# Seven products in place of eight for gate and up, and feed-forward outputs in parts

## The chip, the cores and the metric

The kernel runs on one core of a Trainium2 chip. The metric is the device time of one execution in microseconds. The core has five engines that run side by side: TensorE (PE in the profile, its weight loads PEld) for matrix products, VectorE (DVE) and ScalarE (ACT) for elementwise work, GpSimd (POOL), and SyncE (SP), from whose queue most DMA transfers are issued here. TensorE writes into eight PSUM banks of 128 x 512 floats; everything else lies in SBUF.

## The reference

Two encoder layers over 512 tokens of width 1024, in float32. Each layer is attention and then a feed-forward network with 2816 hidden units; the change touches only the second.

```python
def swiglu(h, w_gate, w_up, w_down):
    return (jax.nn.silu(h @ w_gate) * (h @ w_up)) @ w_down

def reference(x, norm_mix, norm_ffn, w_qkv_a, w_out_a, sink_a, w_qkv_b, w_out_b,
              w_gate, w_up, w_down, norm_final):
    for i in range(DEPTH):
...
        h = rmsnorm(x, norm_ffn[i])
        x = x + swiglu(h, w_gate[i], w_up[i], w_down[i])
    return rmsnorm(x, norm_final)
```

## The kernel before

The state x lies transposed in SBUF: NK = 8 blocks of 128 features by 512 tokens. Every float32 operand of a product is split in two: a high half, rounded by a ScalarE copy, and a low half, the difference, by VectorE (`split`, L91). A product is then three passes, high by high, high by low and low by high (`mm3`, L113), each in matmuls of 128 x 128 weights by 256 tokens. The weights come as units of 128 x 1024 (eight blocks of 128 x 128), and `weight_tiles` (L95) gives each three tiles: wraw, filled by a DMA on SP's queue, and wh and wl, its halves. All three have three buffers (`wpool`, L71), shared by every unit of the kernel.

`swiglu` (L494) runs once a layer, for 22 blocks f of 128 hidden units. For each f `gate(f)` and `up(f)` are units of eight steps (one step is one block of features, six matmuls), with xh and xl, the halves of x times its gain, as moving operand. The norm's factor per token, the row norm["rb"], is applied afterwards: `norm_sums` (L256) adds up squares over features by matmuls with a column of ones and works out the factors, `norm_rows` (L265) turns them into a row by transposes and a copy. `combine(f)` multiplies both products by that row, applies Silu, multiplies, and splits the result into ah and al, which hold all 22 blocks.

Then eight output blocks j: three weight pieces (8, 8 and 6 blocks f), 22 x 6 matmuls into one bank, and the sum with x. In layer 0 `residual` (L278) adds, writes the operands of the next layer's products (`operands`, L211, into xh and xl, here in an order of token classes) and squares x for the next norm (`squares`, L221), whose sum GpSimd keeps. In layer 1 the last j goes through `final` (L450): the last product is made in two halves of 256 tokens, and the norm and the output of the first half (`sums(0)`, `leave(0)`) are put between the matmuls of the second.

The order on TensorE is the order of the program text. On the other engines a planner orders the instructions when the program is built: among those that it finds ready, the earlier in the program goes first; a tile gets a buffer when one of its name is free.

Of the kernel before, what the change touches and what calls it, by code (L numbers as in the profile page):

```python
# [14 lines left out]
S = 512  # L15
# [8 lines left out]
WIN_A = 128  # L24
SLOPES = [float(np.float32(2.0) ** np.float32(-8.0 * (h + 1) / H)) for h in range(H)]
# [39 lines left out]
def trunk(ctx, tc, xT, gains, sink, tabs, qsc, wunits, wv, outT):  # L65
# [385 lines left out]
    def final(product, ps0, ps1, n, j):  # L451
# [30 lines left out]
        for k, _ in enumerate(gen):  # L482
            if k == 5:
                run(sums(0))
            elif k == 12:
                leave(0)
# [7 lines left out]
    def swiglu(u, n):  # L494
        with tc.tile_pool(name="ffn", bufs=2) as pool:
            ah = pool.tile([128, NF, S], F32R, name="ah", bufs=1)
            al = pool.tile([128, NF, S], F32R, name="al", bufs=1)
            part = {}

            def gate(f):  # L500
                def done(ps):
                    part["g"] = ps
                return unit(u + 2 * f, xh, xl, ("mm", "sc")[f % 2], done)

            def up(f):
                def done(ps):
                    part["u"] = ps
                return unit(u + 2 * f + 1, xh, xl, ("tp", "mm")[f % 2], done)

            def combine(f):  # L510
                gs = pool.tile([128, S], F32, name="gs")
# [5 lines left out]
                split(ah[:, f, :], al[:, f, :], us)  # L517

            for f in range(NF):
                if f == 0:  # L520
                    run(gate(0)[1])
                    norm_sums()
                    run(up(0)[1])
                    norm_rows()
                else:
                    run(gate(f)[1])
                    run(up(f)[1])
                combine(f)
            u += 2 * NF
            for j in range(NK):  # L530
                w = []
                for c0 in (0, 8, 16):
                    nk = min(8, NF - c0)
                    w.append(load_unit(wunits[u][:, :128 * nk], (nk, 128)))
                    u += 1
                def product(ps, cols, w=w):
                    for f in range(NF):
                        wh, wl = w[f // 8]
                        mm3(ps[:, cols], wh[:, f % 8], wl[:, f % 8], ah[:, f, cols], al[:, f, cols],
                            f == 0, f == NF - 1)  # L540
                        yield

                ps = bank(("mm", "sc")[j % 2])
                if n < 4:
                    run(product(ps, slice(0, S)))
                    residual(j, ps, n)
                elif j < NK - 1:
# [411 lines left out]
```

## Time and profile before

| what | us |
|---|---|
| median of 3 runs | 1472.62 (1472.39 to 1474.02) |
| the profiled execution | 1473.99 |
| its span, first to last instruction | 1472.3 |
| layer 0, first product of the norm sums ahead of gate and up | 192.48 |
| layer 0, down: first matmul | 427.6 |
| layer 1, last gate and up operands written | 1341.6 |
| layer 1, last down matmul starts | 1460.0 |

The page of the profile gives each engine's busy time and the chain of work that ended last. A row of grouped instructions has line, engine, operation, the tile written and the tiles read, shapes and count; then busy time and mean duration in ns; then the idle time of the engine before them and what ended it. A row of the timeline has start, duration, engine, line and tiles. A row of stretches has the stretch, its length, then busy time and count of PE, PEld, DVE, ACT and POOL, the granted clock of TensorE (1.00 is full), the busy share of the DMA engines and GB/s. A row of one tile has shortest, median and longest duration in ns. A row of DMA issues has the count, the size and the median time to landing.

### The profile page before, as it was taken

Reading aid. Unit: us, or ns where it says so; the run is one execution under the profiler, and the core shown is the slowest. Engines: PE = TensorE matmul, PEld = TensorE weight load, DVE = VectorE, ACT = ScalarE, POOL = GpSimd, SP = SyncE. Lnnn points to the kernel's source line nnn. Section 1 sums busy time; section 2 is a strip of 40 time slices with the busy share of each in tenths; the row PEclk is TensorE's granted clock in tenths of the full one; section 3 lists DMA queues with packets and bytes.
Section 4 is the critical chain, followed back from the end, with each engine's and each line's share of the span. In section 5 each row is a group of like instructions: output and inputs, shape, how many; then the busy total and the mean of one; then the engine's idle time right before and its main releaser. Section 6 shows DMA issues by size and latency. Waiting matters only on the chain.

```text
span 1472.3 us, 29609 instructions
## 1 busy us (share of the span) xinstructions
PE 1453.9 (99%) x12820; PEld 1426.7 (97%) x12820; DVE 732.6 (50%) x1400; ACT 613.9 (42%) x1126; POOL 109.1 (7%) x152
## 2 busy tenths in 40 slices
PE   8999999999999999999999999999999999999997
PEld 8988999999999999999999999999999999999997
DVE  6776544444443345346556556556464444443223
ACT  6776433322323335445545536536343322332221
POOL 3334200000000010000000000000030000000111
PEclk9999999999999999999999999999999999999998
DMA  6110232323223232312212122222132322232331
GB/s 201 58 59 15 87 101 87 101 101 100 94 87 104 94 111 69 101 63 86 79 67 87 58 87 73 72 87 73 44 116 86 101 101 98 90 101 91 96 103 57
DMA packets 38450, 128.29 MB, mean 87 GB/s; under 512 B 4528, under 2 KB 6832, under 8 KB 38320
## 3 DMA queue, kind: packets, MB, share of 16 engines
q1 hardware_dynamic: 36832, 125.08, 25.5%
q8 instruction: 100, 1.64, 0.4%
q10 hardware_dynamic: 1488, 1.33, 0.3%
q14 instruction: 30, 0.25, 0.1%
HBM read 124.29 MB, written 2.10 MB: 86 GB/s over the span
## 4 chain that ended last, share of the span: by engine, by line
PE 94%; DVE 2%; ACT 2%; issue 1%; DMA 0%; POOL 0%; SPq 0%; DVEq 0%; ACTq 0%; POOLq 0%
PE mm L118 51%; PE sc L118 16%; PE psv L118 10%; PE tp L118 8%; PE sc L696 1%; PE sc L637 1%; PE ov L378 1%; PE ov L751 1%; PE sc L140 1%; PE tp L364 1%; PE tp L659 1%; PE ov L678 1%; ACT pr L353 0%; DVE qt L128 0%; PE tp L738 0%
## 5 line engine op out<-in xcount | busy, mean ns | idle before, releaser
L92 ACT ACTIVATE wh<-wraw 128x1024 fp32r<-128x1024 f32 (+3 forms) x239 | 247.6, 1037 | 599.6 <-PE mm L118 252.0
L93 DVE TENSOR_TENSOR wl<-wraw,wh 128x1024 fp32r<-128x1024 f32 (+3 forms) x239 | 290.2, 1215 | 203.3 <-ACT wh L92 202.7
L118 PE MATMUL mm<-xh,wh 128*128 128x256 f32 x1632 | 331.4, 284 | 0.4 <-ACT xh L217 0.4
L118 PE MATMUL mm<-xh,wl 128*128 128x256 f32 x1632 | 321.6, 279 | 2.6 <-DVE wl L93 2.6
L118 PE MATMUL mm<-xl,wh 128*128 128x256 f32 x1632 | 321.7, 279 | 0.7 <-DVE xl L218 0.6
L118 PEld LDWEIGHTS mm<-xh,wh 128*128 128x128 f32 x1632 | 248.5, 189 | 6.3 <-issue 4.8
L118 PEld LDWEIGHTS mm<-xh,wl 128*128 128x128 f32 x1632 | 247.9, 189 | 3.2 <-DVE wl L93 3.2
L118 PEld LDWEIGHTS mm<-xl,wh 128*128 128x128 f32 x1632 | 248.5, 189 | 1.4 <-DVE xl L218 1.3
L232 POOL TENSOR_TENSOR ssum<-ssum,tmp 128x512 f32<-128x512 f32 x34 | 53.7, 1581 | 994.4 <-ACT tmp L228 979.9
L118 PE MATMUL psv<-wh,xh 128*128 128x256 f32 x288 | 82.8, 287 | 0.0
L118 PE MATMUL psv<-wl,xh 128*128 128x256 f32 x288 | 80.4, 279 | 0.0
L118 PE MATMUL psv<-wh,xl 128*128 128x256 f32 x288 | 80.3, 279 | 0.0
L118 PE MATMUL mm<-ah,wh 128*128 128x256 f32 x374 | 74.9, 277 | 0.0
L118 PE MATMUL mm<-al,wh 128*128 128x256 f32 x374 | 74.7, 276 | 0.0
L118 PE MATMUL mm<-ah,wl 128*128 128x256 f32 x374 | 74.7, 276 | 0.0
L118 PE MATMUL tp<-xh,wh 128*128 128x256 f32 x352 | 68.8, 277 | 0.0
L118 PE MATMUL sc<-xh,wh 128*128 128x256 f32 x352 | 68.7, 277 | 0.0
L118 PE MATMUL tp<-xh,wl 128*128 128x256 f32 x352 | 68.6, 276 | 0.0
L118 PE MATMUL tp<-xl,wh 128*128 128x256 f32 x352 | 68.6, 276 | 0.0
L118 PE MATMUL sc<-xh,wl 128*128 128x256 f32 x352 | 68.5, 276 | 0.0
L118 PE MATMUL sc<-xl,wh 128*128 128x256 f32 x352 | 68.5, 276 | 0.0
L118 PE MATMUL sc<-ah,wh 128*128 128x256 f32 x330 | 66.0, 276 | 0.0
(175 smaller groups left out, 2728.6 us busy)
## 6 DMA issues: line engine op xcount, KB each, us to landing
wraw<-wunits SPq DMA_DIRECT2D x192, 512.0 KB, 3.2
wraw<-wv SPq DMA_DIRECT2D x26, 512.0 KB, 3.3
wraw<-wunits SPq DMA_DIRECT2D x16, 384.0 KB, 3.0
x<-xT SPq DMA_DIRECT2D x8, 256.0 KB, 5.1
wraw<-wunits SPq DMA_DIRECT2D x3, 256.0 KB, 5.5
outT<-x ACTq DMA_DIRECT2D x2, 384.0 KB, 2.7
tab<-tabs SPq DMA_DIRECT2D x1, 512.0 KB, 5.5
outT<-x ACTq DMA_DIRECT2D x2, 256.0 KB, 2.2
```

What stands on the lines that cost most here:

```text
L92: nc.scalar.activation(out_h, src, AF.Copy)
L93: nc.vector.tensor_tensor(out_l, src, out_h.bitcast(F32), op=OP.subtract)
L118: nc.tensor.matmul(out[:, cols], a, b[:, cols], start=first and k == 0 and c == 0, stop=last and k == 2, skip_group_check=True)
L140: nc.tensor.matmul(outs[a], qp[a][:, qc], k[a][:, kc], start=first and k is kp, stop=k is low, skip_group_check=True)
L232: nc.gpsimd.tensor_tensor(norm["sum"], norm["sum"], sq, op=OP.add)
L364: nc.tensor.transpose(tp[:, 256 * hf + 128 * i:256 * hf + 128 * i + 128], st["pr"][:, 2 * i + hf, 128 * kb:128 * kb + 128], ident)
L378: nc.tensor.matmul(ov[64 * hf:64 * hf + 64, :256], v0[:, k0 // 128 + kb, vs], st["pt", kb][:, 256 * hf:256 * hf + 256], start=(kb == 0), s ...
L637: nc.tensor.matmul(out, qk["qs", p][a][:, 128 * t:128 * t + 128], kp[k], start=t == ts[0] and k == 0, stop=k == 1, skip_group_check=True)
L659: nc.tensor.transpose(tp[:, (nb * a + kb) * 128:(nb * a + kb) * 128 + 128], st["pr", p, ts][:, a, o + 128 * kb:o + 128 * kb + 128], ident)
L678: nc.tensor.matmul(ov[rows, 128 * t - 64:128 * t + 64], v[:, t - 1 + kb, vs], pt[:, 256 * a + 128 * kb:256 * a + 128 * kb + 128], start=Fa ...
L696: nc.tensor.matmul(ps[a][:, o:o + 128], qk["q", p, 1 + g][rows, cols], qk["k", p, 1 + g][rows, cols], start=(o == 0), stop=True, skip_grou ...
L751: nc.tensor.matmul(ov[rows, 128 * c:128 * c + 128], vals[p // 2, 1 + g][:, c, hv + 64 * a:hv + 64 * a + 64], pts[g][:, 256 * a + 128 * (c ...
```

## The change

The first four f's (`plain`) stay as they were. While they run, the normed input x times gain times norm["rb"] is written out, cut into quarters (B11, B12, B21, B22: the halves of the features by the halves of the tokens), and from these four combinations T1 to T4 are made; B11, B21, B22 and T1 to T4 are split into bh and bl (`input_steps`). For each of the other 18 f's, gate and up together are taken as a 2 x 2 block product (two outputs by two halves of the features, times two halves of the features by two halves of the tokens). `strassen` makes it from seven products of 12 matmuls in place of eight, in two PSUM banks, with copies to SBUF between. Its weights are: the two halves of the gate unit (1 and 2), the sums 4 and 6, of which each is one plain load and one adding DMA issued by GpSimd, the sums 5 and 7, added by VectorE from these, and the second half of the up unit (3). `strassens` lays the products of successive f's into each other.

The hidden outputs no longer stand side by side: ah and al hold 3 blocks, and xh and xl, free after the plain f's, hold 8. So the f's are taken in parts, (0-10), (11-18), (19-21) in layer 0 and (0-10), (11-21) in layer 1, and after each part its down products are added to x. The weights of the down products are laid out by part. Some steps of a part's first down product are put between the last products of the part.

```diff
+PARTS = ((0, 11), (11, 19), (19, NF)), ((0, 11), (11, NF))
...
-            if k == 5:
+            if k == 4:
                 run(sums(0))
-            elif k == 12:
+            elif k == 10:
                 leave(0)
...
-            ah = pool.tile([128, NF, S], F32R, name="ah", bufs=1)
-            al = pool.tile([128, NF, S], F32R, name="al", bufs=1)
+            ah = pool.tile([128, 3, S], F32R, name="ah", bufs=1)
+            al = pool.tile([128, 3, S], F32R, name="al", bufs=1)
...
+            def input_steps():
...
+                        nc.vector.scalar_tensor_tensor(raw[k][:, j % 4, :], x[:, j, cols], g_sb[:, n - 1, j:j + 1],
+                                                       norm["rb"][:, cols], op0=OP.mult, op1=OP.mult)
...
+                steps = [lambda j=j: normed(j) for j in range(NK)]
+                steps += [lambda: parts(B11), lambda: less(T1, B11, B12), lambda: parts(B21), lambda: parts(T1),
+                          lambda: less(T2, T1, B22, -1.0), lambda: parts(T2), lambda: less(T3, B22, B12),
+                          lambda: parts(T3), lambda: less(T4, T2, B21, -1.0), lambda: parts(T4), lambda: parts(B22)]
+                return steps
+
+            def loads(f):
+
+                g, v = wunits[u0 + 2 * f], wunits[u0 + 2 * f + 1]
+                sums = pool.tile([128, 1024], F32, name="w64")
+                nc.sync.dma_start(sums[:, 0:512], g[:, 0:512])
+                nc.sync.dma_start(sums[:, 512:1024], v[:, 512:1024])
+                for k in range(2):
+                    nc.gpsimd.dma_start(sums[:, 512 * k:512 * k + 512], v[:, 0:512], accum_op=OP.add)
+                raw = wpool.tile([128, 1024], F32, name="wraw")
+                nc.sync.dma_start(raw, g)
+                last = pool.tile([128, 512], F32, name="w3")
+                nc.sync.dma_start(last, v[:, 512:1024])
+                return raw, sums, last
+
+            def weights(raw, sums, last):
...
+                halves((wpool, "wh", "wl"), (1, 2), raw)
+                far = pool.tile([128, 1024], F32, name="w57")
+                nc.vector.tensor_tensor(far[:, 0:512], sums[:, 512:1024], raw[:, 0:512], op=OP.add)
+                nc.vector.tensor_tensor(far[:, 512:1024], far[:, 0:512], raw[:, 512:1024], op=OP.add)
+                halves((pool, "h57", "l57"), (5, 7), far)
+                halves((wpool, "wh", "wl"), (6, 4), sums)
+                halves((pool, "h3", "l3"), (3,), last, 512)
+                return w
...
+                def s0():
+                    v["a"], v["g"] = bank("mm"), pool.tile([128, S], F32, name="gs", bufs=3)
+                    product(v["a"][:, one], w[1], B11, True)
+                    nc.scalar.activation(v["g"][:, one], v["a"][:, one], AF.Copy)
...
+                def s6():
+                    product(v["a"][:, one], w[6], T3, False)
+                    v["u"] = pool.tile([128, S], F32, name="us")
+                    nc.scalar.activation(v["u"][:, two], v["a"][:, one], AF.Copy)
+                    nc.vector.tensor_tensor(v["u"][:, two], v["b"][:, two], v["u"][:, two], op=OP.add)
...
+                def s11():
+                    product(v["b"][:, two], w[7], B22, False)
+                    g, t = v["g"], v["u"]
+                    nc.vector.tensor_tensor(g, v["b"], g, op=OP.add)
+                    nc.scalar.activation(g, g, AF.Silu)
+                    nc.vector.scalar_tensor_tensor(t[:, one], v["a"][:, one], -1.0, g[:, one], op0=OP.mult, op1=OP.mult)
+                    nc.vector.scalar_tensor_tensor(t[:, two], t[:, two], -1.0, g[:, two], op0=OP.mult, op1=OP.mult)
+                    split(*place(f), t)
...
+            def strassens(fs, ws, fill, early):
+
+
+                order = sorted((7 * i + at, i, at) for i in range(len(fs)) for at in (0, 1, 3, 5, 6, 9, 11))
+                steps = {}
+                for _, i, at in order:
+                    f = fs[i]
+                    if at == 0:
+                        steps[i] = strassen(f, ws.pop(f))
+                    steps[i][at]()
+                    if at == 1 and i + 1 < len(fs):
+                        ready(f + 1, min(f + 2, fs[-1]))
+                    if i == len(fs) - 1 and at >= 6:
+                        for _ in range(3):
+                            if early:
+                                early -= 1
+                                next(fill)
+
+            def down(j, fs, first):
...
+                w = []
+                for c0 in range(0, len(fs), 8):
+                    m = min(8, len(fs) - c0)
+                    w.append(load_unit(wunits[first + j * len(range(0, len(fs), 8)) + c0 // 8][:, :128 * m], (m, 128)))
+                return gen
...
+            gen = up(0)[1]
+            for _ in range(5):
+                next(gen)
+            norm_rows()
+            run(gen)
+            combine(0)
+            steps = input_steps()
+            ws = {}
+            for f in range(1, plain):
+                for k, (_, gen) in enumerate((gate(f), up(f))):
+                    for i, _ in enumerate(gen):
+                        if i % 2 and steps:
+                            steps.pop(0)()
+                    if f == plain - 1 and k == 0:
+                        ready(plain, plain + 1)
                 combine(f)
...
+            for p, (f0, f1) in enumerate(parts):
+                fs = list(range(f0, f1))
+                pieces = -(-len(fs) // 8)
+                gens = {0: down(0, fs, at)}
+                ps = bank("tp")
+                fill = gens[0](ps, slice(0, S))
+                strassens([f for f in fs if f >= plain], ws, fill, len(fs) - 1)
+                for j in range(NK):
+                    if j:
+                        gens[j] = down(j, fs, at)
+                        ps = bank(("mm", "sc")[j % 2])
+                        fill = gens[j](ps, slice(0, S))
+                    if j == NK - 1 and f1 < NF:
+                        ready(f1, f1 + 1)
...
-    nc = _bacc.Bacc("TRN2", target_bir_lowering=False, num_devices=1)
+    nc = _bacc.Bacc("TRN2", target_bir_lowering=False, num_devices=1, dynamic_dma_scratch_size=4096)
```

`ready(f, ahead)` issues `loads` up to ahead and calls `weights(f)`.

131 lines of the change are left out of this document (91 added, 40 removed).

## The prediction

> **What bounds the kernel now.** I read the page's busy shares and chain first, then the busy time by stage, because the change touches only the two feed-forward stages.
>
> ```profile
> span 1472.3 us, 29609 instructions
> ...
> PE 1453.9 (99%) x12820; PEld 1426.7 (97%) x12820; DVE 732.6 (50%) x1400; ACT 613.9 (42%) x1126; POOL 109.1 (7%) x152
> ...
> PE 94%; DVE 2%; ACT 2%; issue 1%; DMA 0%; POOL 0%; SPq 0%; DVEq 0%; ACTq 0%; POOLq 0%
> ```
> ```profile
> 204.00:427.00 223.00, 223.00 (x1970) 223.00 (x1970) 103.26 (x123) 67.39 (x82) 0.00 (x0) 1.00 0.29 97
> 427.00:547.00 120.00, 120.00 (x1062) 120.00 (x1061) 41.77 (x41) 36.69 (x39) 9.60 (x6) 1.00 0.29 95
> ```
>
> TensorE has 12820 matmuls and as many weight loads and is never idle in a feed-forward stage: in 204 to 427 us (gate and up) it is busy 223.00 of 223.00 us at full clock, and in 427 to 547 (down) 120.00 of 120.00. So 1970 matmuls in 223.00 us make **113.2 ns** each, and whatever removes one there saves that much, as long as nothing else becomes late. VectorE is busy 46% of the first stretch (103.26), ScalarE 30%. They are the cover that the change spends.
>
> **The products removed.** Plain gate and up take 16 x 3 x 2 = 96 matmuls of 256 columns for one f; seven products of 4 x 3 take 84. Every matmul already has a weight load of its own, so another stationary operand each time costs nothing new. 12 x 113.2 ns = 1.36 us for each of 18 f's in 2 layers: **-48.9 us**. The down matmuls stay the same in number.
>
> **VectorE before the first seven-product f.** Prices:
>
> ```profile
> L93 DVE TENSOR_TENSOR wl<-wraw,wh 128x1024 fp32r<-128x1024 f32 x41 | 50.1, 1223 | 4.8 <-ACT wh L92 4.8
> L92 ACT ACTIVATE wh<-wraw 128x1024 fp32r<-128x1024 f32 x41 | 43.8, 1067 | 140.1 <-issue 73.2 <-PE sc L118 32.0 <-PE mm L118 31.0
> ...
> L93 DVE TENSOR_TENSOR al<-us,ah 128x512 fp32r<-128x512 f32 x21 | 14.4, 686 | 0.7 <-ACT ah L92 0.7
> L516 DVE TENSOR_TENSOR us<-us,gs 128x512 f32<-128x512 f32 x20 | 13.9, 693 | 2.1
> L514 ACT ACTIVATE gs<-gs 128x512 f32<-128x512 f32 x21 | 12.9, 614 | 0.0
> L92 ACT ACTIVATE ah<-us 128x512 fp32r<-128x512 f32 x20 | 12.7, 635 | 12.7 <-DVE us L516 12.7
> ```
> ```profile
> L382 ACT ACTIVATE oh<-ov x16: 362/367/387, 58.5 to 153.6; 128x256 fp32r<-128x256 f32 x16
> L383 DVE TENSOR_TENSOR ol<-ov,oh x16: 406/424/426, 58.9 to 154.0; 128x256 fp32r<-128x256 f32 x16
> ```
>
> A 1024-wide two-input operation is 1.22 us, a 512-wide one 0.69, a 256-wide one 0.42. All the new input work waits for the row norm["rb"]. This is where that row stands now:
>
> ```profile
> 192.48 0.94 PE L236 MATMUL ssq<-ones,ssum 128*128 128x1 f32 x8
> 198.83 0.60 PE L270 MATMUL rrow<-ident,rstd 128*128 128x128 f32 x4
> ```
> ```profile
> 198.85 1.06 ACT L92 ACTIVATE wh<-wraw 128x1024 fp32r<-128x1024 f32 x1 [3.82 <-issue]
> 199.81 0.58 ACT L273 ACTIVATE rb<-rrow 128x512 f32<-128x512 f32 x1
> ...
> 204.74 1.07 ACT L92 ACTIVATE wh<-wraw 128x1024 fp32r<-128x1024 f32 x1 [0.91 <-PE sc L118]
> ```
> ```profile
> 204.92 0.69 DVE L513 TENSOR_TENSOR gs<-sc,rb 128x512 f32<-128x512 f32 x1 [0.36 <-PE sc L118]
> 205.84 1.23 DVE L93 TENSOR_TENSOR wl<-wraw,wh 128x1024 fp32r<-128x1024 f32 x1 [0.23 <-ACT wh L92]
> ```
>
> up(0) starts at 193.4; the transposes now come after five of its eight steps (5 x 6 x 113 ns = 3.4 us), so at 196.8, and the copy ends 1.6 us later at most (198.83 to 200.39 today): rb is there at about 198.1. A unit is 48 matmuls, 5.43 us. up(3) is due at 193.4 + 5.43 + 0.6 + 5 x 5.43 = 226.6, which leaves VectorE 28.5 us. Ahead of up(3)'s own split stand, in the order in which the code gives them: three combines (3 x 0.69 + 0.69 = 2.76, together 8.3), four splits (4.9, up(3)'s among them), 16 scalings of 256 columns (6.8), four differences and seven splits of 1024 (11 x 1.22 = 13.4), and the weights of f = 4: three splits and a half (4.35) and two 512-wide sums (1.38), 5.7. Together 39.1, an overrun of **10.6 us a layer, +21.2**. If the planner lets up(3)'s split pass the weights of f = 4, it is 4.9 a layer, +9.8; I take the program order. ScalarE has some 20 us in that stretch and isn't late.
>
> So long a wait also lowers the clock:
>
> ```profile
> 552.88 0.95 PE L236 MATMUL ssq<-ones,ssum 128*128 128x1 f32 x8
> 554.08 1.05 PE L236 MATMUL ssq<-ones,acca 128*128 128x1 f32 x8 [0.26 <-POOL acca L837]
> ```
> ```profile
> 554.00:556.00 2.00, 1.92 (x15) 1.92 (x16) 2.00 (x4) 1.98 (x4) 0.03 (x1) 0.90 0.04 8
> 556.00:558.00 2.00, 2.00 (x11) 2.00 (x11) 2.00 (x5) 1.27 (x1) 0.00 (x0) 0.50 0.00 0
> 558.00:560.00 2.00, 2.00 (x16) 2.00 (x15) 1.86 (x6) 0.21 (x1) 0.00 (x0) 0.74 0.00 0
> ```
>
> One such dip loses 2 x (0.10 + 0.50 + 0.26) = 1.7 us. One a layer: **+3.4**.
>
> **The weight buffers.** wh and wl have three buffers, shared by plain units, down pieces and now two of the four weight splits of each f. The rows of 198.85 and 204.74 show how they are given out: ScalarE takes the buffer when TensorE ends a unit (at 198.85 up(0) has ended, gate(1) and up(1) hold the other two, so this split is for gate(2), two units or 10.9 us ahead). A tile is filled as early as a buffer comes free, in the order of the program. Now down(0, ...) is called before strassens(...), and it loads all pieces of its j at once. In a part of 11 f's these are two (8 + 3), and they are held until the fill at the part's end. They take the buffers of up(3) and of raw(4), and **one buffer is left** for raw(f) and sums(f) in turn. sums(f) has time: after s1 it has three products (4.1 us) and needs 2.3. raw(f+1) has none: its buffer is freed by s6(f), and s0(f+1) is the very next product. From the rows: release at 204.74, low half there at 207.07, 2.33 us, less two matmuls that need only the high half (0.23): 2.1 us. It meets f = 5 to 10 in both layers and 12 to 21 in layer 1's second part: 22 x 2.1 = **+46.2**. Parts of one piece (11 to 18, 19 to 21 in layer 0) keep two buffers and don't wait. From below this term is 0 (a rival); from above each stall trips a clock dip too, 22 x 1.7 = 37 more. In the rows above, some 2.2 us of one-column matmuls (552.9 to 555.1) were enough for one. I leave it out, since full-width matmuls surround each of these waits. [...]
>
> **Within a seven-product f** VectorE has 4.35 (splits) + 1.38 + 0.42 + 0.69 + 2 x 0.42 + 0.69 = 8.4 us beside 84 x 113.2 ns = 9.5 us, ScalarE 3 x 1.07 + 0.64 + 3 x 0.37 + 0.61 + 0.64 = 6.2. Both fit, at 88% and 65%. The copies that free a PSUM half have two products (2.7 us). I cost them at nothing; without that cover each would cost up to one 1.07 us split ahead of it.
>
> **The adding DMAs** stand in no row. A 512 KB load lands in 3.2 us:
>
> ```profile
> wraw<-wunits SPq DMA_DIRECT2D x192, 512.0 KB, 3.2
> ```
>
> Below: nothing, as the loads run two f's ahead. Above: POOL issues two in a row for each f, so their cost shows when a pair takes longer than an f. I take nothing; traffic rises from 1.0 to 1.5 MB an f, which at 0.29 of the DMA engines for 97 GB/s today is some half. [...]
>
> **Part ends.** After its last product, an f's high half needs 0.69 + 0.61 + 2 x 0.42 + 0.64 and four handovers of 0.1: 3.2 us. The fill covers four f's (0.68 each, 2.7) in parts of 11, one in the part of 8, none in that of 3: 3 x 0.5 + 2.5 + 3.2 = **+7.2**.
>
> **Last part of layer 0.** One j is 18 matmuls, 2.04 us, against ScalarE's row work:
>
> ```profile
> L217 ACT ACTIVATE xh<-x,g_sb 128x512 fp32r<-128x512 f32 x7 | 8.5, 1218 | 0.7
> ...
> L228 ACT ACTIVATE tmp<-x 128x512 f32<-128x512 f32 x6 | 3.8, 633 | 0.0
> ```
>
> 1.22 + 0.63 + 0.50 (384 columns, between 367 and 635 ns) = 2.35 us a j: 8 x 0.31 = **+2.5**.
>
> **The end.** The second half of the last down product has 11 f's (3.7 us), not 22 (7.5):
>
> ```profile
> 1457.65 3.23 DVE L474 TENSOR_TENSOR x<-x,rb 128x256 f32<-128x256 f32 x6 [1.90 <-ACT rb L273]
> 1460.80 0.41 DVE L455 TENSOR_TENSOR x<-mm,x 128x256 f32<-128x256 f32 x1
> ```
>
> The first half's six multiplications (3.23 us) ran beside it; now they start as it ends, and the second half's norm queues behind them. Between 0 and 3.2; I take **+2.0**.
>
> **Sum:** -48.9 + 21.2 + 3.4 + 46.2 + 7.2 + 2.5 + 2.0 = +33.6 against the profiled execution's own 1473.99 us, which is 1.4 above the median of 1472.62: **1506 us**. By itself it reaches from 1487 (VectorE's overrun at 9.8, the end at 0, part ends half) to 1535 (most of the clock dips).
>
> **Rivals.** *The fast one:* the two down pieces get their buffers late, or the f's weights go first, and the 46.2 goes. Then 1472.6 - 12.6 = 1460 us, and 1449 with the short overrun. For it: the pieces are needed last. Against: the rows show buffers taken at once. It decides by whether ScalarE's split of f+1 starts at s6(f)'s end or two products earlier. *VectorE becomes the bound:* beside a working POOL a 256-wide split took 1.50 us:
>
> ```profile
> 9.51 1.53 POOL L232 TENSOR_TENSOR ssum<-ssum,tmp 128x512 f32<-128x512 f32 x1 [0.81 <-ACT tmp L228]
> ```
> ```profile
> 9.83 1.50 DVE L93 TENSOR_TENSOR wl<-wraw,wh 128x256 fp32r<-128x256 f32 x1
> ```
>
> If issuing an adding DMA holds VectorE like that, 1.1 us twice an f, it needs 10.6, not 8.4. Beside the forecast's 11.6 us an f that hides; in the fast case it adds 36 x 1.1 = 40, so 1500. [...] *The adding DMAs are slow:* above 5.8 us each a pair outlasts an f, and each further microsecond costs 2 x 36 = 72: 1578 at 6.8. *It isn't what it says*, so that the seven products run slower than 113 ns: excluded by one weight load per matmul already.
>
> **Chances.** Forecast 0.55; fast 0.27; VectorE 0.08; slow DMAs 0.06; something between within 0.2% 0.04 (about what a measurement of this kernel can tell from no change). Faster 0.27, same 0.04, slower 0.69. The range has to take in the fast case: 1449 to 1535, and the forecast's own is 1487 to 1535.
>
> **What would show it.** Right: TensorE waits on wl or wh about 2 us once per f in f = 5 to 10, none in 12 to 18 of layer 0; one wait of some 10 us ahead of up(3); matmuls at 113 ns. Wrong: f's following at 9.5 us in the parts of 11 (fast case), waits on sums or far behind POOL's DMAs, or VectorE busy throughout.

## The result, and the profile after

The changed kernel takes **1591.21 us** (median of 4 runs, 1589.02 to 1593.59) against 1472.51 for the kernel before in the same job: a ratio of **1.0807**, 95% interval 1.0783 to 1.0831. The forecast was 1506, with a range to 1535; the sign was right, the size 85 us too small. The profiled execution took 1589.02, its span 1587.2.

The page after, its span, the busy time of the engines, the chain of work that ended last, and the DMA issues of the seven-product f's:

```profile
span 1587.2 us, 29686 instructions
...
PE 1486.5 (94%) x12388; PEld 1444.8 (91%) x12388; DVE 891.0 (56%) x1674; ACT 722.3 (46%) x1336; POOL 175.3 (11%) x224
...
PE 10%; DVE 1%; issue 1%; ACT 1%; DVEq 0%; ACTq 0%
...
w<-wunits SPq DMA_DIRECT2D x108, 256.0 KB, 3.6
w<-wunits POOLq DMA_DIRECT2D x72, 256.0 KB, 5.0
```

The chain of work could be followed back over some 13% of the span only, so nothing is read from it. TensorE has 432 matmuls fewer and is busy 32.6 us **longer**; its idle time has grown from 18.4 us (1472.3 - 1453.9) to 100.7. So there are two losses, idle time of 82.3 us and busy time that should have fallen by 48.9 and rose by 32.6. The idle time by what ended it (engine, line and tile that waited, what they waited for, then total us, number, longest):

```profile
PE mm L607 <- ACT wh L94: 23.6, 22, 1.1
PE mm L607 <- DVE wl L95: 22.3, 23, 5.0
PE sc L607 <- DVE us L636: 10.1, 5, 3.0
PE mm L120 <- DVE wl L95: 9.8, 6, 3.5
PE rrow L272 <- DVE rstd L256: 8.8, 4, 3.9
...
PE tp L120 <- ACT ah L94: 3.0, 1, 3.0
PE tp L120 <- ACT xh L94: 2.2, 1, 2.2
```

L607 is the matmul of the seven products. The first row has 22 waits: one ahead of s0 in each of the 22 f's that the prediction named. The same waits in the timeline of the changed kernel:

```profile
251.97 0.39 PE L607 MATMUL mm<-bh,wh 128*128 128x256 f32 x1 [1.03 <-ACT wh L94]
...
253.23 0.39 PE L607 MATMUL mm<-bh,wl 128*128 128x256 f32 x1 [0.76 <-DVE wl L95]
```

TensorE stands for the high half, makes its first matmuls and stands again for the low half. What the waits do to the clock, from the stretches of the changed kernel (PE, PEld, DVE, ACT and POOL busy, then TensorE's granted clock):

```profile
276.00:278.00 2.00, 0.75 (x4) 0.55 (x5) 1.53 (x2) 1.23 (x3) 0.00 (x0) 1.00 0.95 154
278.00:280.00 2.00, 2.00 (x13) 2.00 (x13) 1.03 (x3) 0.29 (x1) 0.00 (x0) 0.62 0.97 168
280.00:282.00 2.00, 2.00 (x12) 2.00 (x12) 0.98 (x2) 0.09 (x1) 0.00 (x0) 0.52 0.48 184
```

Of the 2 us that hold the wait TensorE works 0.75; in the 4 us behind it the clock is 0.62 and 0.52 and 25 matmuls start in place of some 35, a loss of 2 x (0.38 + 0.48) = 1.7 us. In finer stretches every dip of this trace ahead of the last norm is 3.41 us at 0.50, or two or three times as long, and all of them begin on one grid of 3.41 us (those at 278.49, 292.14, 305.80 and 319.45 us are four steps of it apart). Counted in spans of 3.41 us there are 33 ahead of the last norm, 56 us of loss in all, and one in the kernel before. Two stretches of that grid, each with the one behind it:

```profile
251.19:254.60 3.41, 1.87 (x14) 1.67 (x14) 2.08 (x3) 1.00 (x2) 0.00 (x0) 1.00 0.18 46
254.60:258.01 3.41, 3.41 (x32) 3.41 (x31) 0.99 (x1) 2.08 (x3) 0.00 (x0) 1.00 0.34 130
...
275.09:278.50 3.41, 1.57 (x11) 1.17 (x10) 2.43 (x5) 1.85 (x3) 0.67 (x1) 1.00 0.86 130
278.50:281.91 3.41, 3.41 (x18) 3.41 (x18) 1.51 (x3) 0.38 (x1) 0.00 (x0) 0.50 0.68 178
```

Each first stretch holds one wait for wh and wl. In the upper pair a part of the wait lies in the stretch before, so 1.54 us of idle time (3.41 - 1.87) are left, and the clock stays at 1.00; in the lower pair they are 1.84, and it falls to 0.50. Apart from the first 10 us and the one-column matmuls of the norms, a stretch at full clock with 1.64 us of idle time (1425.37 us) or more was followed by a dip in this trace, and one with 1.61 (1282.01 us) or less by none. The wait of the upper pair stands in e18 too, 1.03 us at 251.86 and 0.76 at 253.12, and there the 15 matmuls from 254.42 to 257.62 us come 213 ns apart (3.20 / 15): a dip. By cores, the mean granted clock is 0.961 of the span after and 0.996 before: 0.039 x 1587.2 = 62 us of full clock lost against 0.004 x 1472.3 = 6.

### The profile page after: what moved, and what is told of

The parts are those of the page before. It is cut to its first block, busy times and chain, and to the rows that moved or that the text cites. A ratio compares the mean times of both kernels' runs of the same rounds, so it can differ in the third digit from the quotient of the medians.

```text
span 1587.2 us, 29686 instructions
## 1 busy us (share of the span) xinstructions
PE 1486.5 (94%) x12388; PEld 1444.8 (91%) x12388; DVE 891.0 (56%) x1674; ACT 722.3 (46%) x1336; POOL 175.3 (11%) x224
## 3 DMA queue, kind: packets, MB, share of 16 engines
HBM read 152.60 MB, written 2.10 MB: 97 GB/s over the span
## 5 line engine op out<-in xcount | busy, mean ns | idle before, releaser
L120 PE MATMUL mm<-xh,wh 128*128 128x256 f32 x1256 | 261.9, 290 | 4.9 <-ACT xh L219 3.0
L120 PE MATMUL mm<-xh,wl 128*128 128x256 f32 x1256 | 252.3, 282 | 9.1 <-DVE wl L95 9.1
L120 PE MATMUL mm<-xl,wh 128*128 128x256 f32 x1256 | 252.0, 282 | 3.1 <-DVE xl L220 3.1
L577 POOL DMA_DIRECT2D w<-wunits x72 | 63.2, 976 | 612.0 <-DMA w<-wunits 410.4
L607 PE MATMUL mm<-bh,wl 128*128 128x256 f32 x288 | 90.4, 314 | 22.3 <-DVE wl L95 22.3
L607 PE MATMUL mm<-bh,wh 128*128 128x256 f32 x288 | 88.3, 307 | 23.6 <-ACT wh L94 23.6
L607 PE MATMUL sc<-bh,wh 128*128 128x256 f32 x288 | 90.0, 312 | 0.0
L607 PE MATMUL sc<-bl,wh 128*128 128x256 f32 x288 | 89.2, 310 | 0.0
L607 PE MATMUL sc<-bh,wl 128*128 128x256 f32 x288 | 88.4, 307 | 0.0
L607 PE MATMUL mm<-bl,wh 128*128 128x256 f32 x288 | 86.4, 300 | 0.0
L607 PEld LDWEIGHTS mm<-bh,wh 128*128 128x128 f32 x288 | 60.0, 208 | 28.1 <-ACT wh L94 28.1
L607 PEld LDWEIGHTS mm<-bh,wl 128*128 128x128 f32 x288 | 60.6, 210 | 27.0 <-DVE wl L95 27.0
L607 PE MATMUL mm<-bh,h 128*128 128x256 f32 x288 | 81.7, 284 | 0.0
```

What stands on the lines that cost most here:

```text
L120: nc.tensor.matmul(out[:, cols], a, b[:, cols], start=first and k == 0 and c == 0, stop=last and k == 2, skip_group_check=True)
L577: nc.gpsimd.dma_start(sums[:, 512 * k:512 * k + 512], v[:, 0:512], accum_op=OP.add)
L607: nc.tensor.matmul(out, a[:, j], b[:, j], start=first and j == 0 and i == 0, stop=j == 3 and i == 2, skip_group_check=True)
```

## The experiments

### e1 to e4: the buffers, the adding DMAs, the clock

**e1** fetches the two down pieces of a part's first j only when the fill makes its first step:

```diff
             def down(j, fs, first):
                 def gen(ps, cols):
+                    if not w:
+                        pieces()
...
-                for c0 in range(0, len(fs), 8): ... load_unit(...)
+                def pieces():
+                    for c0 in range(0, len(fs), 8): ... load_unit(...)
+                if j:
+                    pieces()
                 return gen
```

> The changed kernel, with the weight pieces of a part's first down product loaded only where its first step runs, so that they hold no weight buffer while the seven-product f's run. Theory of the buffers: the 22 waits on wh and 22 on wl ahead of s0 (45.9 us in the changed kernel) go, and the clock dips that follow them: an f in layer 0's first part takes 9.5 to 10 us, not 12.3, and the time falls from 1591 by 60 to 90 us, to 1500 to 1530. Rival, the adding DMAs: the chain of plain load, adding load and sums (some 12 us in layer 0's second part, which has no lack of buffers) sets the pace in every part; then waits on us or wl take the place of the old ones, an f stays at 12 us or more, and the time falls by less than 20 us.

**e2** leaves the adding DMAs out:

```diff
-                for k in range(2):
-                    nc.gpsimd.dma_start(sums[:, 512 * k:512 * k + 512], v[:, 0:512], accum_op=OP.add)
```

> The changed kernel without its 72 adding DMAs: the second addend of the sums of weights is left out, all else is as it was. Theory of the buffers: layer 0's second part loses its waits on us (10.1 us, and up to 8 us of clock dips), the parts with two down pieces keep their 22 waits; the time falls by 15 to 25 us, to about 1570. Rival, the adding DMAs set the pace throughout: the waits ahead of s0 go as well, and the time falls by over 60 us.

**e3** puts 18 unused matmuls, 2 us, ahead of s0 in the parts of 11 f's, where TensorE stood idle:

```diff
+                    if at == 0 and i and len(fs) not in (3, 8):
+                        idle = bank("ov")
+                        for k in range(18):
+                            nc.tensor.matmul(idle[:, :256], bh[:, B21, k % 4, :128], bh[:, B11, k % 4], start=True,
+                                             stop=True, skip_group_check=True)
                     if at == 0:
                         steps[i] = strassen(f, ws.pop(f))
```

> The changed kernel with 18 matmuls of 256 columns into an unused PSUM bank put ahead of s0 of every f but the first in the parts of 11 f's, so that TensorE works (2.03 us) through the wait for wh and wl; their result is not used. If the loss beyond the waits is the clock that falls after each wait, the granted clock in layer 0's first part rises from 0.92 to 1.00 and the time falls by 25 to 45 us although 396 matmuls are added. If the clock has nothing to do with the waits, the time stays at 1591 or rises.

**e4** has the edits of e1 and e2 together.

> The edits of e1 and e2 together (late pieces, no adding DMAs; the sums of weights lack their second addend). Both theories: no wait is left within the seven-product f's, an f takes 9.5 us; left are the waits around the norm and the first f's, the part ends and the end, some 30 us with their clock dips: 1455 to 1480. If TensorE still waits within the f's, VectorE's 88% is the bound, which would be a third theory.

| run | edit | us | against after (1591.2) |
|---|---|---|---|
| e1 | pieces late | 1546.99 | -44 |
| e2 | no adding DMA | 1559.94 | -31 |
| e3 | 396 matmuls more | 1571.26 | -20 |
| e4 | e1 and e2 | 1484.70 | -106 |

In e1 the 22 waits on wh and wl are gone, and others stand in their place:

```profile
PE sc L607 <- DVE gs L644: 24.0, 17, 3.3
PE mm L607 <- ACT us L635: 17.2, 16, 1.1
```

TensorE waits here for VectorE's work on the products, which stands behind the sums 5 and 7, which wait for the adding DMA (one such row: 5.62 us idle). In e2 the 22 waits stay as they were (23.6 and 21.2 us) and the waits on us are gone. So there are **two chains of nearly the same length, and each hides the other**: e1 and e2 alone give 75 us, together 106. Neither alone came out as its text expected: e1's 44 us lie between the 20 of its rival and the 60 of its theory, e2's 31 between 25 and 60; e4 ended 5 us above its range. The stretch of 244 to 335 us, f = 5 on in layer 0, in the changed kernel and then in e4:

```profile
244.00:335.00 91.00, 80.02 (x601) 77.58 (x600) 50.46 (x70) 39.10 (x61) 10.45 (x12) 0.92 0.53 133
```
```profile
244.00:335.00 91.00, 90.64 (x768) 90.23 (x767) 55.37 (x79) 42.34 (x66) 0.00 (x0) 1.00 0.36 117
```

601 matmuls in the one, 768 in the other. In e3 the clock of this stretch is 1.00 with the buffers still short, and the time falls by 20 us although 396 matmuls were added (396 x 113 ns = 45 us of work): the dips alone cost at least that. By e3's mean granted clock of 0.977 over 1570.8 us, 36 us of full clock are lost in place of 62. The gain was 5 us less than the least that I had expected.

The adding DMA's chain in the changed kernel, from layer 0's second part, where no buffer is short (timeline; L574 is the plain load, L577 the two adding DMAs, L596 the first sum):

```profile
410.12 0.33 SPq L574 DMA_DIRECT2D w<-wunits  x1
...
410.48 0.38 PE L607 MATMUL sc<-bh,h 128*128 128x256 f32 x1 [3.01 <-DVE us L636]
...
413.79 1.75 POOL L577 DMA_DIRECT2D w<-wunits  x2 [13.32 <-DVE gs L644]
...
419.76 0.69 DVE L596 TENSOR_TENSOR w<-w,wraw 128x512 f32<-128x512 f32 x1 [4.45 <-DMA w<-wunits]
```

The load is issued at 410.12, the two additions from 413.79, when it has landed, and VectorE, 4.45 us idle, has the sum at 419.76: 9.6 us, where an f without waits takes 84 x 118.7 ns = 10. The load isn't two f's ahead: `sums` has two buffers, and the one it needs is held until the f before has been split. On VectorE the sums stand ahead of the work on the products: behind its 4.45 us it makes both sums and two splits, and only at 422.83 the addition to us (L636) that TensorE waits for, 1.23 us until 423.30.

### e5: a third buffer for the sums

As e1, with three buffers for the sums and one for w57; nothing is left out.

```diff
-                sums = pool.tile([128, 1024], F32, name="w64")
+                sums = pool.tile([128, 1024], F32, name="w64", bufs=3)
...
-                far = pool.tile([128, 1024], F32, name="w57")
+                far = pool.tile([128, 1024], F32, name="w57", bufs=1)
```

> e1 with three buffers for the sums of weights in place of two (the combinations T1 to T4 take them too; the tile far has one buffer, so that SBUF holds it). Theory of the chain: the adding DMAs cost only because the plain load under them starts when the buffer of two f's before comes free, one f ahead; with three buffers it starts one f earlier, VectorE no longer waits on them, and the time comes near that of e4, which has no adding DMAs: 1485 to 1495. Rival: the adding DMAs are slow by themselves or hold VectorE while they are issued; then the time stays above 1515 and VectorE's rows are longer than 1.23 us or wait on the DMAs as before.

Measured: 1494.07, ratio 1.0148 (1.0108 to 1.0188). With the adding DMAs in place, the time is 9 us above that of e4, which has none: within the f's their chain no longer shows among the waits as soon as it starts an f earlier. What is left by the waits of e5:

```profile
PE mm L120 <- ACT wh L94: 15.2, 2, 7.8
...
PE rrow L272 <- DVE rstd L256: 4.7, 2, 3.9
```

The first is ahead of up(3), once a layer: ScalarE stands with the split of f = 4's sums, whose adding DMA is late, ahead of up(3)'s.

### e6 to e10: the order

**e6** lays two products of an f, with different banks, alternately into each other (e5 otherwise); I thought that adds into the same columns right behind each other might be what slows them.

> e5 with the matmuls of two products laid into each other one by one (s0 with s1, s9 of the f before with s5, and s3 with s11 of the f before from its seventh matmul on), so that successive matmuls add into different banks. In e4 a matmul of the seven products starts 120 ns after the one before, in the plain units 113 ns. Theory: the 7 ns are the price of adding into the same 256 columns twice in a row; 60 of 84 matmuls of 31 f's alternate now, so the time falls by some 60 x 31 x 7 ns = 13 us below e5. Rival: the price is that of other weights or operands each time; then the time doesn't fall, or rises by new waits of the copies.

1494.81, the same as e5, and the products still 118 ns apart. **e7** moves the weights of f = 4 behind up(3) in e6's order:

```diff
-                    if f == plain - 1 and k == 0:
-                        ready(plain, plain + 1)
...
+                        if f == plain - 1 and k == 1 and i == 0:
+                            ready(plain, plain + 1)
```

> e6 with the loads and weights of f = 4 asked for after up(3)'s first step and not before it, so that up(3)'s weights go ahead on VectorE and ScalarE and in the buffers. In the changed kernel up(3) waits 4.5 us in layer 0 (1.0 on wh, 3.5 on wl), and the clock falls after it. Theory of the overrun: those waits go in both layers, and with their dips the time falls by 8 to 14 us below e6. Rival: the work is only put off and f = 4 waits as long; then the time stays within 3 us of e6.

1480.28: the row of 15.2 us went, and the time fell by 14.5. **e10** is e5 with the order of e7, f = 4's loads issued at gate(3)'s first step, and the steps of `sums(0)` and `leave(0)` at k = 3 and 8; **e11** has e6's alternation besides.

> e5 (late pieces, three buffers for the sums) with up(3) ahead of the weights of f = 4 as in e7, the loads of f = 4 asked for at the start of gate(3), and the norm sums and the output of the last product's first half one step and two steps earlier; products in the order of the change, one after the other. e7 without its interleaving, and with the wait on the adding DMAs of f = 4 (7.7 us of ScalarE's idle time in layer 0) taken away: 6 to 12 us below e7, so 1468 to 1474, the same as the kernel before within its noise. If the matmul pitch of 120 ns is what is left, TensorE is busy within the seven-product f's without a gap.

> e10 with the products laid into each other as in e6. If interleaving changes nothing, within 3 us of e10; its copies have less cover, so rather above than below.

e10: 1476.30, ratio 1.0022 (1.0013 to 1.0032); e11: 1476.89. e10 is 4 us below e7, less than the 6 to 12 expected. Of the waits on the weight buffers and ahead of up(3) none is left (the largest row of e10 has 5.2 us in two waits; two part ends still cost 3.0 and 2.3), and the kernel, with 432 matmuls less, is still no faster than before. Of the 48.9 us, idle time takes 19 (37.5 against 18.4) and the clock some 10 (0.989 against 0.996); the largest piece left that no wait explains is in the pace of the matmuls themselves.

### e8, e9, e12 to e18: the pace

In the kernel before, gate and up came 113.2 ns apart; the products come 118 to 120 apart. **e8** runs the passes of `mm3` in the kernel before in the order of the products (half by half of the tokens); **e9** there makes a unit's first half of tokens for all features, then the second, so that weights change after three matmuls. **e12** is e10 with the layout of bh and bl changed (block by block); **e13** is e9 with the moving operand read in blocks of 1 KB, one behind the other.

> The kernel before, with the two loops of mm3 changed over: three passes into one half of 256 columns, then three into the other, where it alternated between the halves. Same matmuls, same weights, same operands. If two successive matmuls into the same columns cost some 5 to 7 ns more, two of three matmuls of mm3 with 512 columns (some 10400 in all) pay it: 35 to 50 us slower, 1507 to 1522. If the pitch depends on something else, the time stays at 1472.

> The kernel before, with the gate and up units (all but f = 0) made half by half: all eight blocks of features for 256 tokens, then all eight for the others. Same tiles, weights, operands and count; each block's weights now serve three matmuls in a row, as in the seven products, where they served six. If it is the renewal of weights after three matmuls that makes the seven products' matmuls 118 to 120 ns apart, the 4128 matmuls come 5 to 7 ns later each and the kernel is 20 to 28 us slower (1493 to 1500). If the pitch hangs on the tiles that are read (bh and bl against xh and xl), the pitch here stays at 113 ns and the time within 3 us of 1472.

> e10 with bh and bl laid out block by block (4 x 7 x 256, not 7 x 4 x 256), so that a product's four moving blocks lie 7 KB apart, not 1 KB. If the pitch of 118.7 ns comes from moving blocks that follow each other in memory, it falls to 113.3, which is worth 84 x 36 x 5.4 ns = 16 us: 1458 to 1462, below the kernel before. If it comes from anything else, the time stays within 3 us of e10 (1476).

> e9 with xh and xl read as if their halves lay one after the other: the eight moving blocks of a half follow each other every 1 KB, where they lay 2 KB apart (it multiplies other features than the reference's, the number and the sizes of the matmuls are the same). If blocks that follow each other cost the 5.4 ns, the 4032 matmuls are 22 us slower: 1492 to 1497; otherwise the time stays at 1472.

e8 1471.97, e9 1472.66, e13 1473.33, all with 113.3 to 113.4 ns; e12 1476.48 with 118.7. So neither the order of the passes, nor how often weights change, nor the layout of the moving tile sets the pace. The next clue is in e10's timeline. Here is the first f of its second part (start in us, at 369.12 the eleven matmuls of s1 with wh and wl, from 370.36 the first product with h57, l57):

```profile
369.12 0.28 PE L607 MATMUL sc<-bl,wh 128*128 128x256 f32 x1
...
370.36 0.28 PE L607 MATMUL mm<-bh,h 128*128 128x256 f32 x1
...
371.68 0.28 PE L607 MATMUL mm<-bh,l 128*128 128x256 f32 x1
```

From 369.12 to 370.36 are 11 steps, 113 ns each; from 370.36 to 371.68 also 11, **120** each. The same moving tile, the same form, another stationary tile; behind h57 and l57 the products with wh and wl too come 117 to 118 apart (in e10 48 matmuls from 261.01 us on at 117.7). In the changed kernel 24 matmuls with wh and wl come 113.3 apart from 243.80 us, 12 with h57 and l57 120.0 from 246.52, and 24 with wh and wl 117.8 from 247.96; behind the waits ahead of 251.97 and 253.23 these come 113.8 apart again. In the program's list of tiles wh and wl begin at a multiple of 512 bytes in the partition, all others named here 192 bytes behind one. e14 to e16 move whole groups of tiles by one unused tile:

```diff
e14   with tc.tile_pool(name="ffn", bufs=2) as pool:
+         pool.tile([128, 80], F32, name="shift", bufs=1)        # e16: 16 in place of 80
e15 + wpool.tile([128, 48], F32, name="shift", bufs=1)           # kernel before
e17   bl = pool.tile([128, 7, 4, 256], F32R, name="bl", bufs=1)
+     pool.tile([128, 80], F32, name="shift", bufs=1)
```

> The version of e10 with one unused tile of 320 bytes at the start of the feed-forward's pool, so that every tile there, the stationary tiles h57, l57, h3 and l3 among them, begins at a multiple of 512 bytes in its partition; before, they began 192 bytes behind one, while wh and wl begin at a multiple. Trace of e10: the products s0 and s1 of the first f, with wh and wl stationary and bh moving, come 114 ns apart; from the first matmul with h57 stationary on all come 117 to 120 apart, and TensorE keeps that pace until its next pause. Theory of the start of the stationary tile: products at 113 to 114 ns, 36 x 84 x 5.2 ns = 16 us less, 1460. Rival, that something else in these tiles or in their steps slows them: 118.5 ns and 1476.

> The kernel before, with one unused tile of 192 bytes at the start of the weights' pool: wh and wl begin 192 bytes behind a multiple of 512. Nothing else is changed. Theory of the start of the stationary tile: the feed-forward's matmuls, 6336 in two layers, come 118 to 120 ns apart in place of 113.3, so 30 to 42 us more, 1502 to 1515. Rival: 113.3 ns and 1472.

> As e14, with a shift of 64 bytes: the stationary tiles begin 256 bytes behind a multiple of 512. If a row of 512 bytes has to lie within one multiple, the products stay at 118 to 120 ns and the time at 1476; if a multiple of 256 is enough, 113.3 ns and 1460.

e14 1480.01, with 402 matmuls in 255 to 303 us (48 / 402 = 119.4 ns), e16 1481.64: not faster, so the theory as written fell. But e15, the kernel before with the weights' pool and the tiles allocated behind it moved by 192 bytes, takes **1509.72**, ratio 1.0253 (1.0239 to 1.0267). Two stretches of it, gate and up, then down:

```profile
260.00:420.00 160.00, 160.00 (x1336) 160.00 (x1335) 69.36 (x84) 45.03 (x56) 0.00 (x0) 1.00 0.28 93
460.00:540.00 80.00, 80.00 (x708) 80.00 (x707) 27.90 (x27) 25.08 (x27) 7.99 (x5) 1.00 0.30 96
```

and the same two of the kernel before:

```profile
260.00:420.00 160.00, 160.00 (x1414) 160.00 (x1413) 74.61 (x90) 48.48 (x60) 0.00 (x0) 1.00 0.29 95
460.00:540.00 80.00, 80.00 (x708) 80.00 (x708) 27.91 (x27) 25.03 (x27) 9.60 (x6) 1.00 0.30 98
```

Gate and up went from 160 / 1414 = 113.2 to 160 / 1336 = 119.8 ns; down kept its 708. xh, which lies ahead of the pool, stays where it was, while ah moves along with wh (the expectation's "nothing else is changed" isn't so). So in gate and up xh and wh now begin at the same place modulo 256 bytes, and in down ah and wh are still 192 bytes apart. So in these runs the pace goes with **how far the stationary tile begins from the moving one**, not with where it begins. The pairs by the distance from stationary to moving modulo 256 bytes:

| stationary, moving | distance | ns from start to start |
|---|---|---|
| wh, xh (before, 160 / 1414); wh, ah (e15, 80 / 708) | 192 | 113.2; 113.0 |
| wh, bh (e10), ahead of the first h57; then behind it | 192 | 113; 117 to 118 |
| h57, bh (e10, from 370.36 us) | 0 | 120.0 |
| wh, xh (e15, 160 / 1336); wh, bh and h57, bh (e14, 48 / 402) | 0 | 119.8; 119.4 |
| xh, wh (product psv, before, 30 to 36 us) | 64 | 117.7 |

**e17** moves h57, l57, h3 and l3 of e10 by 320 bytes from bh and bl, and with them the other tiles that lie behind bl, none of which TensorE reads.

> The version of e10 with one unused tile of 320 bytes between bl and the tiles behind it: h57, l57, h3 and l3 now begin at a multiple of 512 bytes, as wh and wl do, while bh and bl stay 192 bytes behind one. In e14 and e16 stationary and moving tile of a product began at the same place modulo 256 bytes, for wh too, and all products came 120 ns apart; in e15 xh and wh began at the same place and came 120 ns apart, while ah and wh, 192 bytes apart, stayed at 113.3. Theory of the distance between the two tiles: all products at 113.3 ns and, with 36 x 84 x 5.2 ns = 16 us less than e10, 1460 to 1462, so 0.7 to 0.9% faster than the kernel before. Rival, that only the tiles wh and wl are fast: 118 ns and 1476.

Measured: **1462.40** (1456.39 to 1467.95), ratio **0.9941** (0.9922 to 0.9960): 0.6% below the kernel before, with an interval clear of 1, and 14 us less than e10. The stretch 255 to 303 of e10, then of e17:

```profile
255.00:303.00 48.00, 48.00 (x406) 48.00 (x405) 34.79 (x51) 26.36 (x44) 7.91 (x10) 1.00 0.75 184
```
```profile
255.00:303.00 48.00, 48.00 (x426) 48.00 (x425) 34.50 (x51) 26.11 (x42) 7.78 (x9) 1.00 0.72 182
```

48 us hold 406 matmuls at 118.2 ns or 426 at 112.7 (the timeline has 113.3 on average from 260 to 285 us). **e18** puts this tile into the changed kernel alone.

> The changed kernel with the unused tile of e17 alone: h57, l57, h3 and l3 begin 192 bytes from bh and bl modulo 256, all waits and their order are left as they are. In e17 the products came 113.3 ns apart with this. Theory: the products at 113.3 ns here too, so 36 x 84 x 5.2 ns = 16 us less, 1575, as the waits on the buffers are set by ScalarE's and VectorE's work behind a product's end and stay. Rival: the waits take up what the products give, since ScalarE, VectorE and the adding DMAs pace an f: 1585 to 1591.

1587.49 (1579.97 to 1592.40), 4 us less, which lies within the spread of the runs: the rival held. Its page and its waits:

```profile
PE 1472.9 (93%) x12388; PEld 1430.1 (90%) x12388; DVE 889.6 (56%) x1674; ACT 723.2 (46%) x1336; POOL 175.3 (11%) x224
```
```profile
PE mm L608 <- DVE wl L95: 24.5, 23, 6.1
PE mm L608 <- ACT wh L94: 23.5, 22, 1.1
PE sc L608 <- DVE us L637: 13.9, 6, 3.7
...
PE sc L608 <- DVE wl L95: 5.7, 5, 1.9
```

TensorE's busy time fell by 13.6 us (1486.5 to 1472.9) and its idle time rose by 12.0 (100.7 to 112.7), with new and longer waits behind VectorE. In the changed kernel the chains take up what the pace gives, and only behind their repair is it worth its 14 us.

## Why the prediction was right in its sign and wrong in its size

**The weight buffers (+46.2): right.** 22 waits were forecast at 2.1 us, in f = 5 to 10 and in layer 1's second part; the trace has 22, 23.6 us for the high half and 21.0 for the low (22.3 less one wait of 1.3 in layer 0's third part). One of the low ones is 5.0 us long where the others are 0.8, because VectorE stood 7.19 us for an adding DMA ahead of that split; without this excess of 4.3 they are 40 in all. e1 took them away with the cause that was named.

**The clock dips behind them (left out): this step failed most.** The words were "I leave it out, since full-width matmuls surround each of these waits". The stretches of 276 to 282 us show the dip behind just such a wait. Lost clock is 62 us after against 6 before, 56 in all, where the sum had 3.4. The size of one dip, 1.7 us, was right, and so was the bound of 37 for these waits: 18 of the 22 are followed by a dip, one of them by two spans (it holds the wait of 5.0), 32 us in all. What the sum and the bound both lacked is the other 14 spans, 24 us, one at the start and the rest behind waits at the norms, up(3), the adding DMAs and the ends of parts and layer, where the sum had two. Here 1.8 us in two pieces were enough when they fell into one stretch of the grid, and over 244 to 335 us the clock is 0.92 with 10.98 us of idle time (91.00 - 80.02). In e1 the same stretch has 6.70 us (91.00 - 84.30), and the clock stays at 1.00. The waits of 1.84 lay just above the 1.64 that was the least with a dip behind it, and it was luck which four of the 22 fell across an edge of the grid.

**The adding DMAs ("I take nothing, as the loads run two f's ahead"): wrong.** They run one ahead, because of the two buffers of `sums`; load, issue and addition take 9.6 us in the row above, and a pair doesn't have to outlast an f, as the rival had it, to be late. Their direct part is 10.1 us of waits on us, the excess of 4.3 above, and an e2 of -31 us; the greater part lay hidden behind the buffer waits (from e1 to e4 they are worth 62). An adding DMA lands 5.0 us after its issue by the row of DMA issues, a plain load of the same 256 KB 3.6. The traffic was mis-added besides: `loads` fetches 1.75 MB an f, not 1.5 (read from HBM: 152.60 MB against 124.29).

**The products (-48.9): two thirds.** "Another stationary operand each time costs nothing new" and the rival "excluded by one weight load per matmul already" were both wrong: one load each, but from tiles that begin 0 bytes (modulo 256) from bh, and these matmuls come 120.0 ns apart. The gain at 118.7 ns is 36 x (96 x 113.3 - 84 x 118.7) = 33 us, 16 less; e18 puts the pace at 13.6 us of busy time in this kernel, part of it clock. The trace of before had a warning that I didn't read: its psv products run at 117.7 (30 to 36 us), not 113.2.

**VectorE ahead of up(3) (+21.2): well under half.** The waits there are 0.97 and 3.54 us in layer 0 and 0.96 and 2.77 in layer 1, 8.2 in all: the planner let up(3)'s split pass part of the weights of f = 4, which I had named with 4.9 and not taken. A new wait came besides, ahead of the transposes that were moved into up(0):

```profile
199.09 0.69 DVE L95 TENSOR_TENSOR l<-w,h 128x512 fp32r<-128x512 f32 x1 [2.14 <-ACT h L94]
...
200.00 1.09 PE L272 MATMUL rrow<-ident,rstd 128*128 128x128 f32 x4 [2.53 <-DVE rstd L256]
```

VectorE stood with an early split of w3 while the norm's factors waited behind it; in layer 1 a wait at the same place is 1.5 us.

**Part ends (+7.2), the last part of layer 0 (+2.5) and the end (+2.0): about right in sum.** The ends of layer 0's parts of 8 and 3 are the waits of 2.2 us on xh and 3.0 on ah, forecast at 2.5 and 3.2; the parts of 11, at 0.5 each, have no wait above 0.2. Behind layer 0's last part TensorE waits 5.0 us in place of 2.5. The tail has this timeline after:

```profile
1575.15 2.80 DVE L476 TENSOR_TENSOR x<-x,rb 128x256 f32<-128x256 f32 x6
...
1578.97 0.66 PE L272 MATMUL rrow<-ident,rstd 128*128 128x128 f32 x2 [3.93 <-DVE rstd L256]
```

The first half's six multiplications run in front of the second half's norm, as forecast: 14.1 us from the last product's addition (1573.06) to the end, 2.6 more than the 11.5 (1460.80 to 1472.3) of before.

**VectorE as the bound: fell.** Its 1024-wide split takes 1.24 us on average over the whole execution, 1.22 in gate and up of before, and none of the 28 splits of this size that ran while GpSimd issued an adding DMA took more than 1.23:

```profile
L95 DVE TENSOR_TENSOR wl<-wraw,wh 128x1024 fp32r<-128x1024 f32 x182 | 226.0, 1242 | 97.3 <-ACT wh L94 96.4
```

**The total.** The sum's waits alone were 79.1 us (33.6 + 48.9 - 3.4) and the idle time grew by 82.3. That they agree is in part luck: the overrun came out 13 us smaller, and the adding DMAs and the row of the norm filled its place. The busy time is off by 81.5 (1486.5 against 1453.9 - 48.9): 56 of clock, of which the sum had 3.4, some 12 to 16 of pace, and a rest of some 10 that no run takes apart. The forecast's own range begins at 1489 and not at 1487, by the terms that it names.

**The fast case** (1460, named as the rival for late pieces) needed not one repair but four: pieces late, the sums' third buffer, the order of f = 4 and of the end, and the distance of the tiles. With all four it is e17's 1462; that this lies beside 1460 is luck, as the sum for the fast case had neither the pace nor these repairs.

## What to carry to other kernels

Where a change holds a buffer longer, count who is denied it, and price the short waits of TensorE with the dip of the clock behind them: add up the idle time in 3.41 us, not the single pause, as two waits with 1.84 us in one such stretch had a dip behind them here. The dips cost 56 us beside 82 of idle time. Two waits of like length on one engine hid one another here (e1 44 us, e2 31, together 106), so take both away in one run before you judge either, and look for what is left in the pace of the matmuls only then. The lead of the sums was set by when their buffer comes free, one f ahead, not by where their load stands in the text, two f's ahead.

## What was unexpected of the hardware

In these runs the pace of the float32 matmuls of 256 columns goes with where the stationary and the moving tile lie relative to one another: 113.2 ns from start to start in the kernel before, at a distance of 192 bytes modulo 256, 119.4 to 120.0 at 0 (e10, e14, e15), 117.7 at 64 in the one product seen there (psv, before). Moving the weights' pool, and what lies behind it, by 192 bytes cost the kernel before 37 us (e15); moving the four stationary tiles by 320 gained e17 its 14. The slower pace also stayed: in the changed kernel matmuls whose own distance is 192 came 117.8 apart behind those at 120.0 (247.96 us), and 113.8 again behind a pause (253.46). That the distance counts modulo 256 is an estimate of mine from these figures: a period of 64 bytes or less can't be, as 0 and 192 differ, one of 128 would put the 117.7 of 64 beside the 113.2 of 192, and one of 512 isn't likely, as e16, where bh begins 256 bytes from a multiple of 512 and wh at one, took 1481.64 us, as slow as e14. Why there is a period, and why the pace stays, no run tells.

The clock's dips ahead of the last norm are of one size in the traces of both kernels: half the clock for 3.41 us, 1.7 us lost, beginning on a grid of 3.41 us whose place differs from trace to trace (counted from the start of the span, 2.66 us before, 2.01 after). In the changed kernel's trace a dip goes with the idle time within a single stretch of that grid, with the border between 1.61 and 1.64 us. A dip went on there for another 3.41 us when its own stretch still held 0.81 us or more of idle time (435.50 us), and ended at 0.32 or less (8.84 us; one-column matmuls aside).
